# The last output-projection group, the second norm and the first MLP blocks in one written order

## The chip, the cores and the metric

The kernel runs on one NeuronCore of a Trainium2 chip. The metric is the device time of one execution in microseconds; the median of three runs stands for a kernel. TensorE (PE) does matrix products and writes PSUM, which has eight banks. VectorE (DVE) and ScalarE (ACT) do elementwise work, GpSimd (POOL) some additions and DMA issues, SyncE (SP) issues most DMAs. Each engine works through its own queue in order and waits on semaphores for the others.

## The reference

One layer of a transformer with two token mixers. For this change only its middle counts:

```python
x = x + g1 * (_merge_heads(o_da, o_mla, subln_w[l], lambda_init) @ w_o[l])
h2 = _modulate(_rmsnorm(x, norm2_w[l]), sh2, s2)
x = x + g2 * _conv_ffn(h2, w_up[l], conv_w[l], conv_b[l], w_down[l])
```

The modulation vectors (`g1`, `sh2`, `s2`, `g2` and others) are products of `silu(c)` with the 12288 columns of `w_ada`. `_conv_ffn` multiplies by `w_up`, passes the gate half through a centred convolution of width 3 over the tokens and a SiLU, multiplies by the other half, and multiplies by `w_down`. All is float32; 512 tokens, width 2048, feed-forward width 5632.

## The kernel before

Activations lie with features on the 128 partitions and the 512 tokens along the free dimension; a tensor of width 2048 is 16 tiles, numbered `kt` or `dt`. Each float32 product is done as three float32r products: an operand is split into a high part (a copy on ACT that rounds) and a low part (the difference, on DVE), and `mm3` (L104 to L109) adds high by high, high by low and low by high. `wblock` loads a block of weights (128 x 1024) on SP and splits it into `wh` and `wl`, of each of which there are three buffers.

**The output projection** (from L1101) has four groups of four output tiles, and in each group eight blocks of weights; one block is 24 matmuls of 512 columns. Groups 0 and 2 sum up in the two big PSUM tiles, groups 1 and 3 in four one-bank tiles. Between the blocks `next_gemv` computes modulation entries: it loads a row of `ada` (1 MB) and sums its product with `silu(c)` in one DVE instruction (L174). After a group, DVE evicts each output tile, scaled and with the residual added (L1120), into `x1`; POOL sends it to DRAM, ACT squares it, and POOL adds the squares into `ss`.

**The second norm** (`token_norm`, L1086) runs once for all 512 tokens behind the last group: ones matmuls sum `ss` and the last four squares over the partitions, and `rstd` (L160) takes the inverse root with two ACT instructions and four on DVE, one behind the other.

**The MLP's first two feature pairs** (`first_pair`, L1189) are done in the plain way: eight blocks of weights (`w_up0`), in the order 0, 4, 1, 5, 2, 6, 3, 7, each with two input tiles `kt`. For each tile, `normed` (L1152) multiplies by the norm on DVE and makes high and low parts for the two token halves; then `classical` multiplies, half by half, into four outputs: 48 matmuls of 256 columns to a block. From the third pair of features on, `w_up` is applied by a Strassen scheme; its fixed operands `t1` to `t4` are sums of normed tiles, built by `sums(j)` (L1165) for eight `j`, with some twelve DVE and ACT instructions each. The third pair itself is done plainly once more, in four jobs "u" (u0 to u3, 48 matmuls of 256 columns each). Then the "p" jobs begin (first at 1084.88 us in the trace), seven to a feature tile.

Up to and with `first_pair` (L1101 to L1205) the order of instructions here is the scheduler's: it may move each engine's instructions against one another. The jobs stand in `tc.manual_schedule`, where each engine's instructions keep the order of the program text. There, weights are split two jobs ahead: `cast(i + 2)` (ACT) and `low(i + 2)` (DVE) follow job `i`. `convolve`, `silu`, `multiply` and `finish` end the first two features in the order that the scheduler chose, beside the u jobs.

Of the kernel before, what the change touches and what calls it, by code (L numbers as in the profile page):

```python
# [17 lines left out]
P = 128  # L18
# [34 lines left out]
def layer_kernel(ctx: ExitStack, tc: tile.TileContext, small, rope, c_row, cc_row, x_t, ctx_t, ada, ada_k,  # L53
# [1009 lines left out]
    aq_ = tc.alloc_tile_pool(name="aq2", bufs=16, side="right", reuse_waits="tile")  # L1063

    def q2k(dt=F32):
        return aq_.tile([P, 512], dt, tag="q2k", name=nm("q2k"))

    wo = tc.alloc_tile_pool(name="wo", bufs=1, reuse_waits="tile")
# [4 lines left out]
    for h in range(16):  # L1073
        hl = a2k(F32R), q2k(F32R)
        split(hl[0], hl[1], oraw[h])
        osp.append(hl)

    def add_square(pool, ss, x, first):
        if first:
            sc.square(ss, x)  # L1080
        else:
            q = pool.tile([P, T], F32, tag="sq", name=nm("sq"), bufs=2)[:, :x.shape[1]]
            sc.square(q, x)
            gp.tensor_tensor(out=ss, in0=ss, in1=q, op=ALU.add)

    def token_norm(pool, ss, last):  # L1086

        n = ss.shape[1]
        po = b_tile()[:, :n]
        pe.matmul(po, ones32, ss, start=True, stop=False)  # L1090
        for i, x in enumerate(last):
            q = pool.tile([P, T], F32, tag="h", name=nm("sq"), bufs=5)[:, :n]
            sc.square(q, x)
            pe.matmul(po, ones32, q, start=False, stop=i == len(last) - 1)
        r = pool.tile([P, T], F32, tag="nr", name=nm("nr"), bufs=1)[:, :n]
        t1, t2 = (pool.tile([P, T], F32, tag="h", name=nm("n"), bufs=5)[:, :n] for _ in range(2))
        rstd(r, po, D, t1, t2)
        return r

    x1, ss = [], wo.tile([P, T], F32, name="ss")  # L1100
    for g in range(4):  # L1101
        if g % 2:
            outs = [b_tile() for _ in range(4)]
        else:
            s0, s1 = s_tile(), s_tile()
            outs = [s0[:, :512], s0[:, 512:], s1[:, :512], s1[:, 512:]]
        for kb in range(8):
            if kb > 2 and g == 0 or g in (1, 2) or kb < 7 and g == 3:
                next_gemv(wo, 1)
            wh, wl = wblock(w_o[g, kb])  # L1110
            order = [(j, i) for j in range(2) for i in range(4)]
            for j, i in sorted(order, key=lambda t: t[1]) if kb == 7 else order:
                kt, o = kb * 2 + j, j * 512 + i * P
                mm3(outs[i], (wh[:, o:o + P], wl[:, o:o + P]), osp[kt], kt == 0, kt == 15)
        for i in range(4):
            dt = g * 4 + i
            xr = wo.tile([P, T], F32, tag="xr", name=nm("xr"), bufs=6)
            nc.sync.dma_start(xr, x_t[dt])
            x = b2k()
            ve.scalar_tensor_tensor(out=x, in0=outs[i], scalar=modx[:, 32 + dt:33 + dt], in1=xr,  # L1120
                                    op0=ALU.mult, op1=ALU.add)
            x1.append(x)
            gp.dma_start(x1_d[dt], x)
            if g < 3:
                add_square(wo, ss, x, dt == 0)
# [5 lines left out]
    wo.release()  # L1131
    ps_b.release()
    ps_s.release()
    nb[0] = 3
    ps_b = ctx.enter_context(tc.tile_pool(name="ps_m", bufs=4, space=PSUM, reuse_waits="tile"))

    ff = tc.alloc_tile_pool(name="ff", bufs=1, reuse_waits="tile")
    hp = tc.alloc_tile_pool(name="hp", bufs=1, side="right", reuse_waits="tile")
    h0, h1 = slice(0, HT), slice(HT, T)
    r = token_norm(hp, ss, x1[12:])
# [3 lines left out]


    hf, hx, t1, t2, t3, t4 = ([None] * KT for _ in range(6))  # L1150

    def normed(kt):  # L1152

        b = modx[:, 48 + kt:49 + kt]
        h = hf[kt] = hp.tile([P, T], F32, tag="h", name=nm("h"), bufs=5)
        ve.scalar_tensor_tensor(out=h, in0=x1[kt], scalar=a2[:, kt:kt + 1], in1=r, op0=ALU.mult, op1=ALU.mult)
        hx[kt] = (a2k(F32R), q2k(F32R) if kt >= 8 else hp.tile([P, T], F32R, tag="h12", name=nm("h12"), bufs=8))
        for t, c in zip(hx[kt], (h0, h1)):
            hh, hl = half(t)
            sc.activation(hh, h[:, c], AF.Identity, bias=b)  # L1160
            ve.scalar_tensor_tensor(out=hl, in0=h[:, c], scalar=b, in1=hh.bitcast(F32), op0=ALU.add, op1=ALU.subtract)

    spare = [tp.tile([P, T], F32R, tag="tp", name=nm("tp")) for _ in range(8)]

    def sums(j):  # L1165

        a, c, b = hf[j], hf[j + 8], modx[:, 56 + j:57 + j]
        d1, d2 = (hp.tile([P, HT], F32, tag="d", name=nm("d"), bufs=2) for _ in range(2))

        def put_away(t, src):  # L1170
            t[j] = q2k(F32R) if t is t1 else spare.pop(0) if spare else b2k(F32R)
            split(*half(t[j]), src)

        ve.scalar_tensor_tensor(out=d1, in0=c[:, h1], scalar=db[:, j:j + 1], in1=a[:, h1], op0=ALU.add, op1=ALU.add)
# [505 lines left out]
```

## Time and profile before

| | us |
|---|---|
| median of three runs | 2394.99 |
| lowest and highest | 2392.95 and 2395.71 |
| the profiled execution | 2392.88 |
| its span in the profile | 2391.1 |

In the profile a line of the timeline gives start and duration in microseconds, the engine, the source line, the operation, output and inputs with their shapes, and in brackets the idle time of the engine ahead of it with what ended that. The view by stretches gives for each stretch its length and every engine's busy time with its number of instructions, then TensorE's granted clock (1.00 is full), the DMA engines' busy share and the rate. In the view by groups the last columns are busy time, mean duration in ns, and idle time ahead with what ended it. TensorE's records overlap: the distance from one to the next counts, not the duration.

### The profile page before, as it was taken

How to read it: one execution, taken by the hardware profiler on the slowest of the kernel's cores; microseconds unless marked ns; L12 is line 12 of the kernel's file. 1: busy time of each engine (PE TensorE's matmuls, PEld its weight loads, DVE VectorE, ACT ScalarE, POOL GpSimd, SP SyncE). 2: the span in 40 equal slices, each digit the busy share in tenths (PEclk: the TensorE clock that was granted, in tenths of full speed). 3: DMA queues.
4: the chain of work that ended last, by engine and by line, in shares of the span. 5: the costliest groups of instructions: out<-in, count | busy, mean ns of one | idle time of the engine just before them, and what ended most of it. 6: DMA issues, size and time to landing. Idle time of an engine off the chain costs nothing.

```text
span 2391.1 us, 32351 instructions
## 1 busy us (share of the span) xinstructions
PE 2331.0 (97%) x12444; PEld 1961.2 (82%) x12444; DVE 1778.5 (74%) x2303; ACT 1100.7 (46%) x1660; POOL 270.2 (11%) x322
## 2 busy tenths in 40 slices
PE   8999999999899999999999999999999999999997
PEld 5787888777677788798888888888888888888887
DVE  5996886798877877697585858575757676767767
ACT  4322322455555622364454545454545454445453
POOL 0011000121100011200101010101010101011113
PEclk9999999999999999999999999999999999999999
DMA  9767777853301289623646464546555545465572
GB/s 382 284 217 279 297 295 282 234 151 110 132 30 49 71 309 359 211 79 125 156 127 150 123 150 128 143 128 142 139 141 138 145 123 151 123 159 123 144 212 76
DMA packets 141515, 407.45 MB, mean 170 GB/s; under 512 B 14881, under 2 KB 31793, under 8 KB 130737
## 3 DMA queue, kind: packets, MB, share of 16 engines
q1 hardware_dynamic: 107584, 300.51, 37.9%
q0 software_dynamic: 32624, 103.83, 18.1%
q8 instruction: 97, 1.59, 0.3%
q10 hardware_dynamic: 1152, 1.05, 0.1%
q14 instruction: 58, 0.47, 0.1%
HBM read 335.86 MB, written 69.48 MB: 170 GB/s over the span
## 4 chain that ended last, share of the span: by engine, by line
PE 85%; DVE 8%; ACT 3%; issue 3%; DMA 1%; POOL 1%; DVEq 0%; SPq 0%; ACTq 0%; POOLq 0%
PE y L1377 13%; PE b L107 10%; PE b L108 10%; PE b L109 10%; PE z L1377 6%; PE y L1379 6%; PE z L1379 3%; PE s L883 3%; PE s L108 3%; PE s L107 3%; PE s L109 3%; PE x L1377 2%; PE x L1379 1%; PE pt L895 1%; PE f L107 1%
## 5 line engine op out<-in xcount | busy, mean ns | idle before, releaser
L1398 POOL DMA_DIRECT2D x_d<-xs x160 | 140.7, 1017 | 1160.4 <-ACT xs L1397 1140.8
L107 PE MATMUL b<-ah,wh 128*128 128x512 f32 (+1 forms) x672 | 259.1, 386 | 0.0
L108 PE MATMUL b<-al,wh 128*128 128x512 f32 (+1 forms) x672 | 259.0, 385 | 0.0
L109 PE MATMUL b<-ah,wl 128*128 128x512 f32 (+1 forms) x672 | 258.0, 384 | 0.0
L1353 DVE TENSOR_TENSOR wl<-rb,wh 128x1024 fp32r<-128x1024 f32 x124 | 151.2, 1220 | 128.7 <-ACT wh L1347 128.7
L1353 DVE TENSOR_TENSOR wl<-wr,wh 128x1024 fp32r<-128x1024 f32 x126 | 153.8, 1221 | 123.0 <-ACT wh L1347 123.0
L1347 ACT CAST wh<-wr 128x1024 fp32r<-128x1024 f32 x126 | 132.3, 1050 | 200.9 <-PE b L108 100.5
L1347 ACT CAST wh<-rb 128x1024 fp32r<-128x1024 f32 x124 | 130.2, 1051 | 191.7 <-PE b L108 116.1
L1353 DVE TENSOR_TENSOR wl<-ws,wh 128x1024 fp32r<-128x1024 f32 x123 | 150.1, 1221 | 89.2 <-ACT wh L1347 89.2
L174 DVE CUSTOM_DVE_ANT_0 ada<-ada,cb,smt 128x2048 f32<-128x2048 f32 x64 | 154.3, 2413 | 50.9 <-DMA ada<-in_ada 50.6
L1347 ACT CAST wh<-ws 128x1024 fp32r<-128x1024 f32 x123 | 128.3, 1043 | 135.7 <-PE b L108 45.4
L109 PEld LDWEIGHTS b<-ah,wl 128*128 128x128 f32 x672 | 126.3, 188 | 25.5
L107 PEld LDWEIGHTS b<-ah,wh 128*128 128x128 f32 x672 | 126.6, 188 | 22.9
L108 PEld LDWEIGHTS b<-al,wh 128*128 128x128 f32 x672 | 126.6, 188 | 22.0
L107 PE MATMUL b<-a2k,wh 128*128 128x512 f32 (+1 forms) x352 | 134.5, 385 | 7.3 <-ACT a2k L1160 5.0
L109 PE MATMUL b<-a2k,wl 128*128 128x512 f32 (+1 forms) x352 | 132.7, 377 | 0.7 <-DVE wl L402 0.6
L80 ACT CAST wh<-wr 128x1024 fp32r<-128x1024 f32 (+2 forms) x64 | 64.3, 1004 | 147.2 <-DMA wr<-in_w_o 45.7
L1377 PE MATMUL y<-b2k,wh 128*128 128x512 f32 x410 | 106.8, 390 | 0.0
L885 DVE TENSOR_REDUCE m<-s 128x1 f32<-128x768 f32 x96 | 90.2, 949 | 20.0 <-PE s L883 19.7
L81 DVE TENSOR_TENSOR wl<-wr,wh 128x1024 fp32r<-128x1024 f32 (+2 forms) x64 | 79.9, 1249 | 29.7 <-ACT wh L80 29.2
L1397 ACT ACTIVATE xs<-b,modx 128x512 f32<-128x512 f32 x160 | 101.0, 680 | 0.1
L210 ACT CAST wh<-wr 128x1024 fp32r<-128x1024 f32 x38 | 40.0, 1052 | 127.8 <-PE b L109 46.3
(536 smaller groups left out, 6080.5 us busy)
## 6 DMA issues: line engine op xcount, KB each, us to landing
rb<-in_w_up SPq DMA_DIRECT2D x123, 512.0 KB, 4.4
ada<-in_ada POOLq DMA_DIRECT2D x52, 1024.0 KB, 6.1
wr<-in_w_dn SPq DMA_DIRECT2D x84, 512.0 KB, 4.0
x_d<-xs POOLq DMA_DIRECT2D x160, 256.0 KB, 6.1
ada<-in_ada SPq DMA_DIRECT2D x28, 1024.0 KB, 6.9
wr<-in_w_up SPq DMA_DIRECT2D x53, 512.0 KB, 4.2
wr<-in_w_f SPq DMA_DIRECT2D x34, 512.0 KB, 5.9
adak<-in_ada_k SPq DMA_DIRECT2D x64, 256.0 KB, 5.4
```

The source lines that it names most:

```text
L81: ve.tensor_tensor(dst_l, src, dst_h.bitcast(F32), op=ALU.subtract)
L107: pe.matmul(out, st[0], mv[0], start=start, stop=False, **kw)
L108: pe.matmul(out, st[0], mv[1], start=False, stop=False, **kw)
L109: pe.matmul(out, st[1], mv[0], start=False, stop=stop, **kw)
L174: ve.tensor_tensor_reduce(out=junk, in0=w, in1=vec, op0=ALU.mult, op1=ALU.add, scale=1.0, scalar=col("b_ada", j), accum_out=dst[:, j:j + 1])
L885: ve.tensor_reduce(out=m, in_=s[:, :TT], axis=AX.X, op=ALU.max, negate=True)
L1347: sc.copy(hi, raw)
L1353: ve.tensor_tensor(lo, raw, hi.bitcast(F32), op=ALU.subtract)
L1377: pe.matmul(o, w[j][0], hs[j], start=start and j == 0, stop=False, skip_group_check=True)
L1379: pe.matmul(o[:, h0], w[j][1], hs[j][:, h0], start=False, stop=j == 7, skip_group_check=True)
L1397: sc.mul(x, po, modx[:, 80 + dt:81 + dt])
L1398: gp.dma_start(x1_d[dt], x, accum_op=ALU.add)
```

## The change

Three parts, all between the output projection and the p jobs.

*Written order.* The output projection's last group, the norm and the first pairs' blocks (now called units 0 to 7) stand in `tc.manual_schedule` for all engines. Seven rows of `ada` are summed within blocks 0 to 5, each row asked for two sums ahead. The weights of the last group, of the units and of u0 and u1 form one list `src8`; a block is cast and split two ahead (`cast8`, `low8`) and its load is asked for three ahead.

*Norm by token halves.* Blocks 6 and 7 of the last group run first for tokens 0 to 255, then for 256 to 511; `squares_of`, `ones_of`, `root_of` and `normed` take a half. Units 0 and 1 also run by halves.

*Places.* The units sum up in banks of the two big PSUM tiles and one more, apart from the last group's four; low parts lie in two pools of eight tiles; scratch tiles come from a pool `xsp`; the ring of the pairs' weights (`rb`) is allocated and first asked for after u2. `sums(j)` is cut into two steps, `first` (four differences on DVE, four copies on ACT) and `second` (four low parts on DVE), and `some(n)` issues the next n of the sixteen steps. `cast(2)` and `low(2)` stand ahead of the convolutions, `cast(3)` behind them.

```diff
+    def out_block(outs, kb, w, c=slice(0, T), skip=True):
+        order = [(j, i) for j in range(2) for i in range(4)]
+        for j, i in sorted(order, key=lambda t: t[1]) if kb == 7 else order:
+            kt, o = kb * 2 + j, j * 512 + i * P
+            mm3(outs[i][:, c], [t[:, o:o + P] for t in w], [t[:, c] for t in osp[kt]], kt == 0, kt == 15, skip)
...
+    def low8(i):
+        ve.tensor_tensor(hl8[i][1], raw8.pop(i), hl8[i][0].bitcast(F32), op=ALU.subtract)
+        load8(i + 3)
...
-    for g in range(4):
+    for g in range(3):
...
+    def normed(kts, *cs):
+        for kt in kts:
+            norm_in(kt, cs)
+        for kt in kts:
+            norm_low(kt, cs)
...
+        def first():
+            d1, d2, d3, d4 = ds[:] = [d for _ in range(2) for d in half(scratch())]
...
+            for t, d in zip((t1, t2, t3, t4), ds):
+                sc.copy(half(t[j])[0], d)
+
+        def second():
+            for t, d in zip((t1, t2, t3, t4), ds):
+                hh, hl = half(t[j])
+                ve.tensor_tensor(hl, d, hh.bitcast(F32), op=ALU.subtract)
...
+        for i in range(6):
+            out_block(outs, i, hl8.pop(i))
+            cast8(i + 2)
+            low8(i + 2)
+            for _ in range(1 + (i == 2)):
+                row_sum()
+                row_load()
+            if i == 2:
+                xrs = [residual(12 + k) for k in range(4)]
...
+        for kb in (6, 7):
+            out_block(outs, kb, hl8[kb], h0)
...
+        cast8(8)
+        low8(8)
+        squares_of(h0)
+        out_block(outs, 6, hl8[6], h1)
+        ones_of(h0)
+        out_block(outs, 7, hl8[7], h1)
+        root_of(h0)
+        normed(pair(0), h0)
+        squares_of(h1)
...
+        fo.append(b_tile())
+        unit(0, (h0,))
+        ones_of(h1)
+        cast8(9)
+        low8(9)
+        normed(pair(1), h0)
+        unit(1, (h0,))
+        cast8(10)
+        low8(10)
+        root_of(h1)
+        normed(pair(0), h1)
+        unit(0, (h1,))
+        normed(pair(1), h1)
+        cast8(11)
+        low8(11)
+        unit(1, (h1,))
+        normed(pair(2), h0, h1)
...
+        for n_ in range(2, 8):
+            unit(n_, (h0, h1))
+            cast8(10 + n_)
+            if n_ < 7:
+                normed(pair(n_ + 1), h0, h1)
+            low8(10 + n_)
+            some((0, 1, 2, 1, 2, 3)[n_ - 2])
...
+        for i in range(2):
+            ready[i] = *hl8.pop(16 + i), None, None
+        cast(2)
+        low(2)
+        for i in range(2):
+            t = convolve(i, fo[2 * i])
+            if i:
+                some(1)
+            acts[i] = multiply(silu(t), fo[2 * i + 1])
+            some(1 - i)
+            finish(t, acts[i])
...
         for i, job in enumerate(jobs[:last]):
             run(i)
+            if i == 2:
+                hp.release()
...
+                rb = Ring(mm, "rb", 3, items_b)
+                rb.pump()
...
-            cast(i + 2)
             if i:
+                cast(i + 2)
+            if i > 2:
                 act_after(i - 1)
                 vec_after(i - 1)
-            low(i + 2)
+            if i:
+                low(i + 2)
+            if i < 4:
+                some((2, 1, 0, 2)[i])
```

More of the change, by code (lines that the diff above doesn't have):

```diff
@@ L1073, in layer_kernel @@
     for h in range(16):
-        hl = a2k(F32R), q2k(F32R)
+        hl = a2k(F32R), q2k(h // 8, F32R)
         split(hl[0], hl[1], oraw[h])
         osp.append(hl)
[L1078 to L1098, printed above, removed]
@@ L1102, in layer_kernel, with load8, cast8 @@
+    raw8, hl8 = {}, {}
+    def load8(i):
+        if i < len(src8):
+            raw8[i] = wraw(src8[i])
+    def cast8(i):
+        hl8[i] = [wp.tile([P, 1024], F32R, tag=g, name=nm(g), bufs=3) for g in ("wh", "wl")]
+        sc.copy(hl8[i][0], raw8[i])
+    def low8(i):
+        ve.tensor_tensor(hl8[i][1], raw8.pop(i), hl8[i][0].bitcast(F32), op=ALU.subtract)
+        load8(i + 3)
+    x1, ss = [], wx.tile([P, T], F32, name="ss")
+    for g in range(3):
         if g % 2:
@@ L1152, in normed @@
[L1152 to L1161, printed above, removed]
```

214 lines of the change are left out of this document (136 added, 78 removed).

## The prediction

> **What bounds the kernel now.** I read the page first, then the stretches around the changed code, then the timeline in the one place where TensorE stops, and last the engines beside it.
>
> ```profile
> PE 2331.0 (97%) x12444; PEld 1961.2 (82%) x12444; DVE 1778.5 (74%) x2303; ACT 1100.7 (46%) x1660; POOL 270.2 (11%) x322
> PE 85%; DVE 8%; ACT 3%; issue 3%; DMA 1%; POOL 1%; DVEq 0%; SPq 0%; ACTq 0%; POOLq 0%
> ```
>
> TensorE is busy 97% of the span and carries 85% of the chain that ended last. So a change can win only where PE stops or runs slowly, and it loses wherever it makes PE stop. The stretches below run from the end of block 5 of the output projection's last group (two blocks before 1001.79) to the first Strassen job.
>
> ```profile
> core 0: us, PE busy (x) PEld busy (x) DVE busy (x) ACT busy (x) POOL busy (x), PEclk, DMA share, GB/s
> 990.91:1001.79 10.88, 10.88 (x49) 9.01 (x48) 4.59 (x5) 2.11 (x3) 1.22 (x3) 1.00 0.35 102
> 1001.79:1012.12 10.33, 4.73 (x12) 1.64 (x10) 6.07 (x9) 4.99 (x9) 0.97 (x2) 0.96 0.41 149
> 1012.12:1061.84 49.72, 49.33 (x386) 49.11 (x387) 48.30 (x103) 29.97 (x64) 0.00 (x0) 0.94 0.22 64
> 1061.84:1084.88 23.04, 23.04 (x193) 23.04 (x193) 17.63 (x30) 11.09 (x18) 0.00 (x0) 1.00 0.45 160
> ```
>
> ```profile
> 1012.10:1018.00 5.90, 5.88 (x27) 5.86 (x28) 5.87 (x14) 3.47 (x9) 0.00 (x0) 0.50 0.00 1
> ```
>
> Three things are to be seen. First, 1001.79 to 1012.12 is the second norm: PE works 4.73 of 10.33 us. Second, right behind it 27 matmuls take 5.90 us at a granted clock of 0.50, so 0.22 us each, where the four "u" jobs run 192 in 23.04 us, 0.12 us each. Third, from 1012.12 to 1061.84 DVE is busy 48.30 of 49.72 us: behind the norm **VectorE has no room**, though PE does not wait for it yet.
>
> PE's bare work from 1001.79 to 1084.88 is 576 matmuls at 0.12 (69.1) and the ones matmuls (4.3: eight records took 3.70, below), together 73.4 of 83.1 us. **9.7 us are lost**, and that is all that can be won.
>
> ```profile
> 1000.63 0.75 DVE L1120 SCALAR_TENSOR_TENSOR b2k<-b,modx,xr 128x512 f32<-128x512 f32 x1 [0.61 <-PE b L109]
> ...
> 1003.39 3.70 PE L1094 MATMUL b<-sq,ones 128*128 128x512 f32 x8 [0.57 <-ACT sq L1093]
> ...
> 1007.13 0.69 ACT L162 ACTIVATE nr<-b,epst 128x512 f32<-128x512 f32 x1 [2.23 <-PE b L1094]
> 1007.85 0.63 ACT L163 ACTIVATE nr<-nr 128x512 f32<-128x512 f32 x1
> 1007.85 0.69 DVE L164 TENSOR_SCALAR n<-b 128x512 f32<-128x512 f32 x1 [3.79 <-ACT nr L162]
> ...
> 1009.96 0.69 DVE L167 SCALAR_TENSOR_TENSOR nr<-n,nr 128x512 f32<-128x512 f32 x1
> 1010.77 1.42 DVE L1156 SCALAR_TENSOR_TENSOR h<-b2k,a,nr 128x512 f32<-128x512 f32 x2
> 1011.55 0.51 ACT L1160 ACTIVATE a2k<-h,modx 128x256 fp32r<-128x256 f32 x1 [3.08 <-DVE h L1156]
> ```
>
> Read downwards this is the stall: the last ones record, two ACT steps and four DVE steps of 0.63 to 0.69 us one behind the other, one norm multiply (0.75), one activation (0.51), and then PE (1012.12).
>
> **The change, part by part.** All times are on the clock of this execution. The zero of the hand schedule is 990.91. An instruction on a busy engine counts by its distance to the next, taken from these rows (DVE first, then ACT).
>
> ```profile
> 1050.54 0.75 DVE L1156 SCALAR_TENSOR_TENSOR h<-b2k,a,nr 128x512 f32<-128x512 f32 x1
> 1051.21 1.22 DVE L1353 TENSOR_TENSOR wl<-wr,wh 128x1024 fp32r<-128x1024 f32 x1
> 1052.35 0.75 DVE L81 TENSOR_TENSOR b2k<-d,b2k 128x256 fp32r<-128x256 f32 x2
> 1053.02 0.48 DVE L1180 SCALAR_TENSOR_TENSOR d<-h,modx,d 128x256 f32<-128x256 f32 x1
> 1053.41 0.48 DVE L1161 SCALAR_TENSOR_TENSOR a2k<-h,modx,a2k 128x256 fp32r<-128x256 f32 x1
> ```
>
> ```profile
> 1020.72 1.05 ACT L80 CAST wh<-wr 128x1024 fp32r<-128x1024 f32 x1 [2.12 <-PE b L108]
> 1021.67 0.71 ACT L80 CAST tp<-d 128x256 fp32r<-128x256 f32 x2
> ```
>
> So on DVE: a 512-wide multiply 0.66, a weight's low part 1.14, a 256-wide low part 0.34 (subtract) or 0.40 (with scalar). On ACT: a weight cast 0.95, a 256-wide copy 0.30.
>
> *Halves on PE.* Blocks 6 and 7 become 96 matmuls of 256 columns for 48 of 512: 96 × 0.12 = 11.52 for 10.88, so +0.64. The ones matmuls are cut in two at the same total. Unit 0 and unit 1 have the same matmuls as before.
>
> *The norm of the first half.* Its eviction and squares lie beside block 6's second half, its chain beside block 7's. No 256-wide row of that chain exists. It lies between half of the full rows (0.35 a step) and the full rows (0.69); I take 0.46 to 0.50, by the 256-wide rows next to it (0.48, 0.51). The first ones end at 1001.7, the chain gives the first activation at 1005.4, and PE has worked up block 7 at 1004.6: **0.9 us of waiting and 0.4 for the low part, in place of 9.7**. The clock stays up.
>
> *What is late next.* The written order puts weight blocks between the norm steps. PE waits again: for the second pair's first half (its multiply stands on DVE behind low8(9), which waits for cast8(9) behind the second half's squares) 0.8 + 0.4; for the first pair's second half (root_of(h1) behind low8(10)) 2.2 + 0.4; for unit 2 (behind cast8(11), which needs unit 0's buffer) 0.9 + 0.4. With the first wait, and 0.4 of short ones, that is 6.4. PE ends unit 7 at 990.91 + 11.52 + 4.27 + 384 × 0.12 + 6.4 = 1059.2, against 1061.84: **−2.6 us**.
>
> *What the moved sums cost.* From here DVE decides. That a written order is kept, waits and all, this kernel's own written part shows:
>
> ```profile
> 1086.55 0.75 DVE L1219 SCALAR_TENSOR_TENSOR t<-y,smt,t 128x511 f32<-128x511 f32 x1 [4.08 <-ACT t L1214]
> ...
> 1088.01 1.21 DVE L1353 TENSOR_TENSOR wl<-ws,wh 128x1024 fp32r<-128x1024 f32 x1
> ```
>
> DVE stood idle 4.08 us for the convolution's input, and the low part written behind it came after it all the same. By that rule: at 1025.9 DVE has issued pair 2's norm. Up to unit 7's sums it still has five pairs (2 × 0.66 + 4 × 0.40 = 2.92 each, 14.6), six lows (6.8), five first halves of a sum (0.40 × 3 + 0.34 and 0.12 of dependence, 1.66 each, 8.3), four second halves (4 × 0.34, 5.4): 35.1 us, and some 2.4 us of waits for ACT. It is done at 1063.4, **4 us behind PE**. Then the written order is cast(2), convolution 0, a half sum, convolution 1, a half sum, the second activation, two more half sums, and only then cast(3), which job u3 needs. The scheduler's order in the old kernel had that weight's low part here:
>
> ```profile
> 1064.42 1.28 ACT L1226 ACT_TABLE_LOAD   x1
> 1065.72 0.63 ACT L1226 ACTIVATE t<-t 128x512 f32<-128x512 f32 x1
> ...
> 1074.35 1.23 DVE L1353 TENSOR_TENSOR wl<-wr,wh 128x1024 fp32r<-128x1024 f32 x1 [0.87 <-ACT wh L1347]
> ```
>
> ```profile
> L1236 DVE TENSOR_TENSOR al<-t,ah 128x512 fp32r<-128x512 f32 x2 | 1.4, 688 | 0.7 <-ACT ah L1232 0.7
> L1230 DVE TENSOR_TENSOR t<-t,b 128x512 f32<-128x512 f32 x2 | 1.4, 681 | 0.0
> L1219 DVE SCALAR_TENSOR_TENSOR t<-b,smt,t 128x511 f32<-128x511 f32 x1 | 0.7, 746 | 0.0
> L1353 DVE TENSOR_TENSOR wl<-wr,wh 128x1024 fp32r<-128x1024 f32 x3 | 3.7, 1225 | 0.9 <-ACT wh L1347 0.9
> ```
>
> It was 4.7 us ahead of u3 (1061.84 + 3 × 5.76 = 1079.1). In the new order DVE's work between 1063.4 and low(3) is: low(2) 1.1, four convolution steps 3.0, two products 1.3, two low parts 1.3, two first halves of a sum 3.3, two second halves 2.7: 12.7. DVE waits for ACT's casts, the table load (1.28), the two silus, the copies and the reuse of the one tile t, each 0.7 to 2.1: 8.0. So low(3) starts at 1084.1, its cast ends just before. PE asks for u3 at 1059.2 + 17.3 = 1076.5 and **stands 7.5 us, then 1.0 for the low part: +8.5**. Queued behind cast(3) on ACT are cast(4) and cast(5), and behind low(3) on DVE low(4), the weight sum and the last sum; the p jobs get them just in time, so I add nothing there (at most 1.1).
>
> *The clock.* The old stall had 5.03 us of idle PE and then 5.9 us at 0.50. 7.5 us of idle should do the same to u3: 5.9 / 2 = 2.95 us, of which about 1 lies in the wait for low(3): +2.0. The shorter waits (up to 2.2) I take at nothing; if one of them dropped the clock it would cost up to 2.95.
>
> By the Trainium skill ("TensorE: Matmul & The Clock Gate", Part 1) the clock halves after an idle window of about 3.4 us and returns after about as long a busy one. By its figure the u3 wait would cost an estimated 1.7 us in place of 2.95; the trace's 5.9 us at 0.50 is longer, and the measurement is used above.
>
> *Banks.* Evicting the first half reads a bank into which PE wants to write the second half. An eviction is 0.75 at full width; four end by 997.3, and PE comes back to each bank later than that (996.7 + 0.36 for each next bank, the first bank done 2 us earlier). Cost 0; if DVE began only after block 7's whole first half, under 1 us. The Trainium skill ("PSUM — Partial Sum Buffer", on bank collisions) forbids two engines on one bank at once, which speaks against halves in a bank; no wait of this kind is in the trace.
>
> *Rows.* Seven row sums lie in blocks 0 to 5.
>
> ```profile
> 978.77 2.35 DVE L174 CUSTOM_DVE_ANT_0 ada<-ada,cb,smt 128x2048 f32<-128x2048 f32 x1 [3.24 <-DMA ada<-in_ada]
> ```
>
> With a low part a block of 5.44 us holds 1.14 + 2.4 of DVE, so even a wait of 3.24 in front of a sum is caught up within two blocks, and weights are split two blocks ahead. So 0. The loads of u2 and u3 are asked for as low8(15) and low8(16) free their buffers, more than a unit (5.76) ahead of their casts. The pairs' ring moves behind u2 on SP's queue:
>
> ```profile
> rb<-in_w_up SPq DMA_DIRECT2D x123, 512.0 KB, 4.4
> ```
>
> Its first use is the weight sum behind u3's start; asked for within u2, three loads at 4.4 us land before DVE, late as it is, comes to them: 0, and without that lateness up to some 3 us.
>
> **Sum**: −2.6 + 8.5 + 2.0 = **+7.9 us**. The profiled execution took 2392.88 (span 2391.1), low in the three runs (2392.95 to 2395.71); on their median, 2394.99, it gives **2402.9**.
>
> **Rivals.** *Faster.* The halves hide the norm and DVE, which starts its norm 6.4 us earlier (1004.4 for 1010.77), brings low(3) in by 1076.5. Without waits on ACT it would: 1084.1 less its waits (8.0 here, 2.4 in the units, some 5 before) is below 1070. Then −2.6 stands, which is no change yet; with the waits at the start half as long too (3.2 for 6.4) it is −5.8: about 2389; at the very best −9.7 + 0.64, 2386. For it speaks that DVE idled only 1.4 us in the 49.7 us above; against it, that there the scheduler mixed the sums freely, and the written order does not. It decides at low(3) = 1076.5.
>
> *No change.* DVE is not late, or by 2 to 5 us at most with PE's clock up, and this eats the gain at the front: 2392 to 2398.
>
> *Worse.* A short wait at the front drops the clock as well (+2.95) or the p jobs wait too (+1.1, DVE having little room behind): 2404 to 2407.
>
> *Not what it says.* If the rows or weights came late, PE would stop inside blocks 0 to 5, where it never stops now; it would be seen there, and would add to the forecast.
>
> **How the numbers follow.** The forecast (2399 to 2404 by itself) has 0.48, the worse case 0.12, no change 0.20, faster 0.20. About 0.2%, 4.8 us, is what a measurement of this kernel can tell from no change. Range 2387 to 2408: it takes in most of the faster case and all of the worse one.
>
> **What would show it.** Right: in the new profile PE waits under 1.5 us ahead of unit 0, in all 5 to 7 us before unit 2; PE ends unit 7 near 1059; then one wait of 6 to 9 us ahead of u3 on ACT's cast or DVE's low, with a granted clock near 0.5 behind it; DVE waits for ACT in the convolutions. Wrong: no wait ahead of u3, or low parts coming before the sums on DVE, or PE idle for rows in the last group.

## The result, and the profile after

| | before | changed |
|---|---|---|
| median, us (four runs each) | 2395.35 | 2412.93 |
| lowest and highest, us | 2392.95, 2396.84 | 2410.95, 2415.26 |
| span of the profiled execution, us | 2391.1 | 2409.2 |

The changed kernel is slower: ratio 1.0075, 95% interval 1.0057 to 1.0092. The direction was forecast, the size was not: 2402.9 was forecast, and 2412.93 lies outside the range of 2387 to 2408. Of the runs below, one execution of f1 (3894.68 us) and one of i1 (5388.43 us) were far slower than the rest and are left out of all figures.

On the page of the changed kernel the busy shares of the engines (its first line) are what they were. TensorE is busy 8.5 us longer, since it runs slowly in places, and no other engine became the bound of the whole. The loss has to be looked for in the stretch.

```profile
PE 2339.5 (97%) x12502; PEld 1971.3 (82%) x12502; DVE 1780.0 (74%) x2315; ACT 1101.2 (46%) x1666; POOL 268.7 (11%) x322
```

The stretch that the change touches runs from the first matmul of block 6 to job p(4,0), from where the two kernels do the same. Its ends, from the timelines, first of before, then of after:

```profile
990.91 0.39 PE L107 MATMUL b<-a2k,wh 128*128 128x512 f32 x1
...
1104.36 2.00 PE L1377 MATMUL y<-a2k,wh 128*128 128x512 f32 x8
```

```profile
991.34 0.28 PE L107 MATMUL b<-a2k,wh 128*128 128x256 f32 x1
...
1122.76 1.55 PE L1485 MATMUL y<-a2k,wh 128*128 128x512 f32 x6
```

It is 113.45 us before and 131.42 us after: **+18.0**, and the spans differ by 18.1. So the whole loss is in here. This also gives a sharper measure than the total: what lies ahead of block 6 takes 990 to 1001 us from one profiled execution to the next, whatever is changed behind it, while two executions of one kernel agree in the stretch to 0.1 us (experiment h2 below, whose clock is full throughout). The experiments are therefore compared by the stretch first. Where a wait drops the clock, the stretch is less exact: what the same code takes can differ by 1.4 us from one execution to the next (e2 below).

Where the 18 us went is seen in the timeline of TensorE, cut to the matmuls that had to wait (in brackets the idle time ahead and what ended it), and in the view by stretches with the granted clock (the column behind POOL).

```profile
1005.75 0.38 PE L107 MATMUL s<-a2k,wh 128*128 128x256 f32 x1 [0.59 <-ACT a2k L1165]
...
1017.72 0.38 PE L107 MATMUL s<-h,wh 128*128 128x256 f32 x1 [2.38 <-ACT h L1165]
...
1079.22 0.55 PE L107 MATMUL z<-a2k,wh 128*128 128x256 f32 x1 [6.33 <-DVE t L1341]
...
1106.41 2.07 PE L1485 MATMUL y<-b2k,wh 128*128 128x512 f32 x4 [7.70 <-ACT m L1409]
```

```profile
1017.72:1022.50 4.78, 4.64 (x24) 4.45 (x25) 2.54 (x6) 1.26 (x3) 0.00 (x0) 0.66 0.00 0
...
1026.12:1061.21 35.09, 34.95 (x289) 34.76 (x289) 32.64 (x66) 19.71 (x41) 0.00 (x0) 1.00 0.28 89
...
1079.22:1092.96 13.74, 13.74 (x96) 13.74 (x97) 8.57 (x16) 3.73 (x7) 0.00 (x0) 0.82 0.39 140
...
1106.41:1111.58 5.17, 5.17 (x16) 4.40 (x17) 4.67 (x6) 2.62 (x3) 0.00 (x0) 0.52 0.21 53
```

Three waits, at unit 0's second half, at u2 and at p(3,2), and behind each of them a granted clock below 1. The old wait of 5.03 us at the norm is gone. Unit 7 ends 69.87 us behind the start of block 6 (1061.21), where it was 70.93: the norm's part wins 1.1 us. Job p(3,0) starts at 1092.96, 101.6 us behind block 6, for 93.8 before (in the old timeline its first matmul starts at 1084.71, not at 1084.88): 7.8 us have been lost by then. The other 10.2 go at p(3,2).

Below is the chain that ends at p(3,2), from the timelines of VectorE, ScalarE and SyncE's queue (SPq), in order of time.

```profile
1084.31 2.00 ACT L1455 CAST wh<-wr 128x1024 fp32r<-128x1024 f32 x2
1085.38 1.23 DVE L1461 TENSOR_TENSOR wl<-wr,wh 128x1024 fp32r<-128x1024 f32 x1 [1.95 <-ACT wh L1455]
...
1086.64 0.33 SPq L1366 DMA_DIRECT2D wr<-in_w_up  x1
...
1087.02 1.37 SPq L1366 DMA_DIRECT2D rb<-in_w_up  x3
...
1091.67 1.23 DVE L1425 TENSOR_TENSOR ws<-rb,wr 128x1024 f32<-128x1024 f32 x1 [2.58 <-DMA rb<-in_w_up]
...
1094.21 1.05 ACT L1455 CAST wh<-rb 128x1024 fp32r<-128x1024 f32 x1 [7.91 <-DMA rb<-in_w_up]
1095.30 1.22 DVE L1461 TENSOR_TENSOR wl<-rb,wh 128x1024 fp32r<-128x1024 f32 x1 [2.40 <-ACT wh L1455]
...
1100.92 1.04 ACT L1455 CAST wh<-ws 128x1024 fp32r<-128x1024 f32 x1 [1.79 <-DVE ws L1428]
...
1105.78 0.58 ACT L1409 COPY m<-y 128x512 f32<-128x512 f32 x1
```

Read it downwards. low(3) runs at 1085.38. When it has read its buffer, SyncE may refill that buffer (the `wr` load at 1086.64). The three loads of the pairs' ring stand behind this load in SyncE's order and go out at 1087.02. ScalarE then stands 7.91 us and VectorE 2.58 us for their data, and everything that is written behind them (a sum, the second weight sum, the third convolution, the copy `m` that frees the tile of p(3,2)) comes as much later. In the old kernel the same loads went out 15 us earlier, and ahead of the refills:

```profile
1071.91 1.81 SPq L1259 DMA_DIRECT2D rb<-in_w_up  x3
...
1073.82 0.87 SPq L1259 DMA_DIRECT2D wr<-in_w_up  x2
```

My theory, at this point: two chains, one behind the other. The written order of VectorE and ScalarE makes cast(3) and low(3) late, and u2 or u3 waits; and through SyncE's order the late low(3) makes the pairs' loads late, and p(3,2) waits. The rival for u2: the wait names `t` of L1341, the second product, and u2's output tile lies in the PSUM bank (4) in which that product still reads `fo[3]`; so a bad bank alone may be the cause. The `z` tile that the change asks for first, to move u2's tile one slot on, is written and read by nothing, and u2 waits as if it were not there.

### The profile page after: what moved, and what is told of

Same layout as the page of the kernel before. It is cut to its first block, busy times and chain, and to the rows that moved or that the text cites. A ratio compares the mean times of both kernels' runs of the same rounds, so it can differ in the third digit from the quotient of the medians.

```text
span 2409.2 us, 32462 instructions
## 1 busy us (share of the span) xinstructions
PE 2339.5 (97%) x12502; PEld 1971.3 (82%) x12502; DVE 1780.0 (74%) x2315; ACT 1101.2 (46%) x1666; POOL 268.7 (11%) x322
## 4 chain that ended last, share of the span: by engine, by line
PE 84%; DVE 8%; ACT 4%; issue 2%; DMA 1%; POOL 1%; SPq 0%; DVEq 0%; ACTq 0%; POOLq 0%
PE y L1485 13%; PE b L107 10%; PE b L108 10%; PE b L109 10%; PE z L1485 6%; PE y L1487 6%; PE s L108 3%; PE s L109 3%; PE s L107 3%; PE z L1487 3%; PE s L883 3%; PE x L1485 2%; PE x L1487 1%; PE pt L895 1%; PE f L107 1%
## 5 line engine op out<-in xcount | busy, mean ns | idle before, releaser
L109 PE MATMUL b<-ah,wl 128*128 128x512 f32 (+1 forms) x672 | 258.0, 384 | 0.0
L174 DVE CUSTOM_DVE_ANT_0 ada<-ada,cb,smt 128x2048 f32<-128x2048 f32 x57 | 135.8, 2385 | 48.6 <-DMA ada<-in_ada 48.4
L109 PEld LDWEIGHTS b<-ah,wl 128*128 128x128 f32 x672 | 126.3, 188 | 25.6
L107 PE MATMUL b<-a2k,wh 128*128 128x512 f32 (+1 forms) x336 | 128.8, 383 | 0.1
L109 PE MATMUL b<-a2k,wl 128*128 128x512 f32 (+1 forms) x336 | 125.9, 375 | 0.0
L80 ACT CAST wh<-wr 128x1024 fp32r<-128x1024 f32 (+2 forms) x50 | 49.6, 991 | 111.2 <-DMA wr<-in_w_o 60.3
L1485 PE MATMUL y<-b2k,wh 128*128 128x512 f32 x328 | 85.7, 404 | 11.2 <-ACT m L1409 11.2
L107 PE MATMUL s<-a2k,wh 128*128 128x512 f32 (+1 forms) x240 | 89.7, 374 | 1.5 <-ACT a2k L1165 1.5
```

What stands on the lines that cost most here:

```text
L107: pe.matmul(out, st[0], mv[0], start=start, stop=False, **kw)
L109: pe.matmul(out, st[1], mv[0], start=False, stop=stop, **kw)
L174: ve.tensor_tensor_reduce(out=junk, in0=w, in1=vec, op0=ALU.mult, op1=ALU.add, scale=1.0, scalar=col("b_ada", j), accum_out=dst[:, j:j + 1])
L1485: pe.matmul(o, w[j][0], hs[j], start=start and j == 0, stop=False, skip_group_check=True)
```

## The experiments

"Stretch" in the tables is from unit 0's start to job p(4,0): 117.0 us in the changed kernel. From block 6 to unit 0's start they take 14.4 us (h2's two executions 14.6 and 14.7), so that the old kernel's 113.45 from block 6 stands against 99.0 here. Runs of one table row are compared with runs of the kernel before on the same chip.

### The causes taken one by one

**e1: the bank.**

```diff
-                    live["s"] = [b_tile(g_, 2) for g_ in "yz"]
+                    live["s"] = [b_tile("y", 2), b_tile()]
```

> Only u2's and u3's output tile goes from bank 4 (where fo[3], the second gate product's input, still lies) to bank 0. Theory (the order of ScalarE and VectorE sets the end: cast(3) and low(3) stand behind both convolutions, and the pairs' loads behind low(3) on SyncE's queue): the 6.3 us wait ahead of u2 goes, a wait of 7 to 8 us ahead of u3 takes its place, the wait of 7.7 us ahead of p(3,2) stays, and the time stays within 2 us of the changed kernel, 2411 to 2415. Rival (the bank that u2 shares with fo[3] is the cause of the loss there): the wait goes and nothing comes in its place, 2404 to 2407.

**e2: SyncE's order.** The load that low(3) sets free is asked for behind the three loads of the pairs' ring.

```diff
-        def low(i):
+        def low(i, hold=False):
...
-                if done:
+                if done and not hold:
                     done()
...
                 rb.pump()
+                ready[3][3]()
...
-                low(i + 2)
+                low(i + 2, i == 1)
```

> Only the load that low(3) sets free (it refills the ring of the u and w11 weights) is asked for behind the three loads of the pairs' ring on SyncE's queue, not ahead of them. Theory (the pairs' loads are late because they stand on SyncE's queue behind a load that waits for low(3)): they are issued some 4 to 5 us earlier, the wait of 2.6 us ahead of the first weight sum goes, the wait ahead of p(3,2) falls from 7.7 to 2 to 3 us, and the time by 4.5 to 7 us, to 2406 to 2408.5. Rival (VectorE's own order, the sums and low parts that stand ahead of the third convolution, holds p(3,2) back, and the loads wait beside it): p(3,2) still waits 6 us or more, 2411 to 2414.

**e3: cast(3) ahead of the second convolution**, with u2's tile away from `fo[3]`: the pool of the jobs' PSUM tiles is opened ahead of the last group, whose outputs, `po` and `fo` are now tiles of that pool.

```diff
+        outs = [b_tile(g_, 2) for g_ in "zzyy"]
...
+        po, *fo = [b_tile(*t) for t in (("b", 3), ("b", 3), ("b", 3), ("x", 1))]
...
+        fo.append(b_tile("z", 2))
...
+        run(0)
+        run(1)
         for i in range(2):
             t = convolve(i, fo[2 * i])
...
             finish(t, acts[i])
+            if not i:
+                cast(3)
+                low(3)
```

> The cast and low part of u3's weight go ahead of the second convolution, and the output tiles lie so that u2 shares no bank with fo[3]. Theory (u2 and u3 wait only for these two things): PE runs from unit 7 through u3 without a wait over 1 us and at full clock, u3 ends 8 to 10 us earlier, p(3,2) still waits 6 to 8 us for the copy behind the third convolution, since VectorE's work in front of it is the same, and the time falls by 6 to 9 us, to 2404 to 2407. Rival (VectorE is short of time as a whole, not in a bad order): what u3 gains is lost again ahead of p(3,2), whose wait grows to 12 us or more, and the time stays at 2411 to 2414.

**e4: the front.** The weight blocks of units 1 and 2 leave the places ahead of norm steps.

```diff
         out_block(outs, 6, hl8[6], h1)
+        cast8(9)
+        low8(9)
         ones_of(h0)
...
         ones_of(h1)
-        cast8(9)
-        low8(9)
...
-        cast8(10)
-        low8(10)
         root_of(h1)
         normed(pair(0), h1)
         unit(0, (h1,))
+        cast8(10)
+        low8(10)
```

> In the norm's part the cast and low part of unit 1's weight go ahead of the first half's root (ScalarE waits for the ones matmuls there), and those of unit 2's weight behind unit 0's second half. Theory (two weight blocks written ahead of norm steps make the waits of 0.4 and 2.4 us, and the 2.4 us wait halves the clock): PE waits at most 1 us in any place from block 6 to unit 2, the granted clock stays at 1.00, unit 7 ends 3.5 to 5.5 us earlier, and since everything behind is shifted the time falls by as much, to 2407.5 to 2409.5. Rival (the waits only move to unit 1's second half and unit 2): unit 7 ends less than 1.5 us earlier, 2411.5 to 2414.

| | median, us | ratio to before (95%) | stretch, us | wait at u2, u3 | wait at p(3,2) |
|---|---|---|---|---|---|
| e1_bank | 2415.02 | 1.0076 (1.0059 to 1.0094) | 116.6 | 2.49, then 2.55 + 0.75 | 6.83 |
| e2_ring | 2408.02 | 1.0048 (1.0030 to 1.0065) | 108.2 | 6.34, none | 3.16 |
| e3_cast3 | 2409.29 | 1.0046 (1.0027 to 1.0064) | 109.2 | none | 7.50 |
| e4_front | 2409.96 | 1.0061 (1.0041 to 1.0080) | 116.0 | 6.42, none | 7.45 |

*e1* decides between theory and rival. TensorE's waits in its timeline:

```profile
1079.01 0.35 PE L107 MATMUL b<-a2k,wh 128*128 128x256 f32 x1 [2.49 <-DVE t L1332]
1089.04 0.39 PE L107 MATMUL b<-a2k,wh 128*128 128x256 f32 x1 [2.55 <-ACT wh L1455]
1090.30 0.58 PE L109 MATMUL b<-a2k,wl 128*128 128x256 f32 x1 [0.75 <-DVE wl L1461]
```

u2 still waits a little, now for the first convolution, whose input lies in its new bank, and u3 waits for cast(3) and low(3), 3.3 us in place of the 7 to 8 expected. The stretch wins 0.4 us. The bank is what the trace names, and it costs next to nothing by itself: behind it stands the order, ready to take the same time.

*e2*: the pairs' loads go out at 1067.58 in its trace, 71.5 us behind block 6 where it was 95.7, and no instruction waits for them any more:

```profile
1067.58 2.60 SPq L1366 DMA_DIRECT2D rb<-in_w_up  x3
1090.07 0.33 SPq L1366 DMA_DIRECT2D wr<-in_w_up  x1
```

```profile
1104.67 2.12 PE L1485 MATMUL y<-b2k,wh 128*128 128x512 f32 x8 [3.16 <-ACT m L1409]
```

The wait at u2 is as it was, the one at p(3,2) falls from 7.70 to 3.16, and the clock stays at 1.00 behind it. The stretch is 8.8 us shorter, but not all of this is the edit's. From p(3,0) to p(4,0) it takes 22.98 us for 29.80, which is 6.8 less. Another 1.4 were won ahead of unit 2, in code that the edit leaves alone: behind the same wait of 2.38 us the clock stayed at 1.00 in this execution (last section), and unit 0's second half and unit 1's took 7.02 us for 8.40. The last 0.6 came behind the u2 wait, at a clock of 0.87 for 0.82. So of the 18.0 us lost, 6.8 were the place of one load on one queue. The ratio says about the same (1.0048 for 1.0075, 6.5 us), and the median came within the 2406 to 2408.5 expected.

*e3*: u2 and u3 do not wait, p(3,0) waits 1.26, and p(3,2) waits 7.50, though the pairs' loads went out 24.6 us ahead of it and nothing waits for them:

```profile
1079.89 1.37 SPq L1370 DMA_DIRECT2D rb<-in_w_up  x3
```

```profile
1104.47 3.78 PE L1489 MATMUL y<-b2k,wh 128*128 128x512 f32 x8 [7.50 <-ACT m L1413]
```

That is the second half of the theory: VectorE's work ahead of the third convolution is late by itself. The stretch falls by 7.8, as expected, 0.5 of it at the front, where unit 0's second half waits 1.72 us for 2.38 (`po` has a tile of its own here, see e4). The median shows less (1.0046), and block 6 started 6 us later in this execution than in the changed kernel's.

*e4* missed. The 0.39 us wait at unit 1 went, the 2.4 us wait stayed to the hundredth, unit 7 ended 1.3 us earlier, and the stretch won 1.0 us, where 3.5 to 5.5 were expected. The timeline shows why: ScalarE's first root step of the second half

```profile
1012.61 0.48 ACT L162 ACTIVATE nr<-s,epst 128x256 f32<-128x256 f32 x1 [3.74 <-PE s L109]
```

waits for L109, a matmul of a unit, though its sums are ready when the ones matmuls end, at 1008.89 + 1.89 = 1010.78. `po` and `fo[0]` are the two halves of one PSUM tile, `s`, and the step waits for all that is written to this tile ahead of it in the program, unit 1's first half too.

### The front with po in a tile of its own, and both together

**f1** is e4's front with e3's tiles (`po` alone in a tile, u2 away from `fo[3]`). **f2** is f1 with e3's early cast(3).

> The weight blocks are moved as in e4_front, and the sums of squares (po) have an output tile of their own, not one half of the tile whose other half takes unit 0's first result; u2's tile lies apart from fo[3] too. Theory (ScalarE's first root step of the second half waits for the tile that unit 1's first half writes, not only for its own sums): that step starts within 0.3 us of the last ones matmul, the wait of 2.4 us ahead of unit 0's second half falls to 0.3 to 0.8 us, the granted clock stays at 1.00 behind it, unit 7 ends 4.5 to 6 us earlier counted from unit 0's start, and the stretch from unit 0's start to job p(4,0), 117.0 us in the changed kernel and 116.0 in e4_front, falls to 111 to 112.5. Rival (the root step waits for something else, the order on its queue or the ones matmuls themselves): the wait stays at 2 us or more and the stretch at 115 to 116.5.

> The front of f1_front_po and the earlier cast of u3's weight of e3_cast3 together. If the front and the middle are separate losses they add: 111.8 expected for the front, 7.8 less for the middle, so 103 to 105.5 us from unit 0's start to p(4,0), with one wait of 6 to 8 us left ahead of p(3,2). Rival (VectorE has no room, so that PE's earlier units only wait for it later): 107 or more, and the wait ahead of p(3,2) grows to 10 us.

| | median, us | ratio to before (95%) | stretch, us | wait at unit 0's second half | at u3 | at p(3,2) |
|---|---|---|---|---|---|---|
| f1_front_po | 2410.82 | 1.0055 (1.0033 to 1.0078) | 113.0 | 0.59 | 6.81 + 0.46 | 6.48 |
| f2_all | 2403.22 | 1.0030 (1.0015 to 1.0044) | 106.1 | 0.59 | none | 7.49 |

In f1 the root step follows the ones matmuls at once, and the clock stays up where the changed kernel had 0.66:

```profile
1018.67 1.89 PE L1273 MATMUL b<-sq,ones 128*128 128x256 f32 x8
```

```profile
1020.60 0.48 ACT L162 ACTIVATE nr<-b,epst 128x256 f32<-128x256 f32 x1 [1.96 <-PE b L1273]
```

```profile
1024.01:1029.00 4.99, 4.71 (x32) 4.11 (x33) 3.90 (x8) 3.14 (x5) 0.00 (x0) 1.00 0.22 71
```

So the wait had two causes, either of which was enough for most of it: the shared tile alone made 2.38 us (e4), the weight blocks ahead of the root alone 1.72 (e3). f1 missed its sum all the same: unit 7 ended 3.9 us earlier (4.5 to 6 expected), and the stretch is 113.0 (111 to 112.5 expected), since u3 now waits 7.3 us in two pieces for cast(3) and low(3). f2 lies between theory and rival (106.1, for 103 to 105.5 or 107 and more): front (4.0) and middle (7.8) nearly add up to the 10.9 that it wins, and the wait at p(3,2) stays. With everything mended that is in one place, the written order still loses 7 us against the kernel before.

### The rest left to the scheduler

**h1** keeps f1's front by hand up to unit 1. Units 2 to 7, the sums and the first two convolutions stand outside `manual_schedule`, and the written order starts at u0 as in the kernel before.

```diff
-        for n_ in range(2, 8):
-            unit(n_, (h0, h1))
...
+    for n_ in range(2, 8):
+        if n_ > 3:
+            cast8(8 + n_)
+            low8(8 + n_)
+        for j, kt in enumerate(pair(n_)):
+            if n_ > 2:
+                normed([kt], h0, h1)
+            if n_ % 2 == 0:
+                some(2)
+            for i in range(4):
+                o = j * 512 + i * P
+                classical(fo[i], kt, [t[:, o:o + P] for t in hl8[8 + n_]], False, n_ == 7 and j == 1)
+    some(4)
...
+    for i in range(2):
+        t = silu(convolve(i, fo[2 * i]))
+        acts[i] = finish(t, multiply(t, fo[2 * i + 1]))
```

**h2** is h1 with four sums among the units in place of six, one in each of units 4 to 7, and the other four behind the convolutions.

```diff
-            if n_ % 2 == 0:
+            if (n_, j) in ((4, 1), (5, 1), (6, 1), (7, 1)):
                 some(2)
...
         acts[i] = finish(t, multiply(t, fo[2 * i + 1]))
+        some(4)
```

**h3** is h1 with the low parts of the sums on GpSimd, and **h4** has both edits.

```diff
-                ve.tensor_tensor(hl, d, hh.bitcast(F32), op=ALU.subtract)
+                gp.tensor_tensor(out=hl, in0=d, in1=hh.bitcast(F32), op=ALU.subtract)
```

> The front of f1_front_po by hand up to unit 1; units 2 to 7, the sums, the two convolutions and u0's and u1's weights are left to the scheduler, and the written order begins at job u0 as in the kernel before. Theory (the written order of sums, weights and convolutions makes the loss behind the front; VectorE has the time, given the scheduler's mixing): PE does not wait over 1 us anywhere from unit 2 to p(4,0), the stretch from unit 0's start to p(4,0) is 93 to 96 us (92.2 in the kernel before, whose norm stands ahead of it), and with the 9.7 us at the norm cut to some 3 the kernel is faster than before by 3 to 7 us, ratio 0.997 to 0.999. Rival (VectorE, idle for only 1.4 of 49.7 us in the units of the kernel before, is the bound as soon as PE's norm wait goes): PE waits 3 to 6 us spread over units 2 to 7, the stretch is 97 to 100 us, and the time equals before within 0.1%.

> As h1_hybrid (102.3 us from unit 0's start to p(4,0), waits of 1.2 to 1.5 us ahead of four units, VectorE busy 5.00 of 5 us from 1030 to 1060), but two sums fewer stand among the units: they come behind the convolutions, where VectorE had idle time in h1_hybrid (2.56 and 3.92 of 5 us busy from 1080 to 1090). Theory (VectorE has no room in the units and PE waits for it there; it has room behind them): the waits ahead of the units fall below 0.5 us each, the stretch to 96 to 99 us, the ratio to before to 0.999 to 1.001. Rival (VectorE is short over the whole stretch to p(4,0)): the waits come back in jobs u0 to p(3,3), the stretch stays at 101 us or more.

> As h1_hybrid, with the 32 low parts of the sums (0.34 us each on VectorE, 10.9 us in all) done by GpSimd, whose 256-wide two-input operation takes 0.80 us in the kernel before and which has nothing else to do there. Theory (VectorE's work is the bound from the norm to the p jobs): PE's four waits of 1.2 to 1.5 us go, the stretch from unit 0's start to p(4,0) falls from 102.3 to 94 to 97 us, the kernel is faster than before by 2 to 5 us, ratio 0.998 to 0.999. Rival (the waits come from the order and from latency between ScalarE and VectorE, not from VectorE's load): the stretch stays at 100 us or more.

> h2_later and h3_pool together. Theory (VectorE's load): no more than 1 us better than the better of the two, since either makes room enough: 94 to 96 us from unit 0's start to p(4,0), ratio 0.9975 to 0.999. Rival (GpSimd, 32 x 0.80 = 25.6 us of work, becomes late when the sums start later): p(3,2) to p(3,5) wait for low parts on GpSimd, 98 us or more.

| | median, us | ratio to before (95%) | stretch, us |
|---|---|---|---|
| h1_hybrid | 2399.82 | 1.0022 (1.0009 to 1.0034) | 102.3 |
| h2_later | 2389.82 | 0.9965 (0.9953 to 0.9977) | 95.7 |
| h3_pool | 2403.92 | 1.0026 (1.0013 to 1.0039) | 104.5 |
| h4_both | 2398.53 | 1.0009 (0.9998 to 1.0021) | 101.2 |

*h1* missed what the theory expected, 93 to 96, and what the rival did. Its units and its u jobs, from the view by stretches (behind PE and PEld the third busy time is VectorE's):

```profile
1024.42:1074.91 50.49, 44.20 (x336) 42.48 (x337) 48.85 (x108) 29.77 (x64) 0.00 (x0) 0.97 0.23 71
1074.91:1097.95 23.04, 23.04 (x194) 23.04 (x193) 15.77 (x22) 9.98 (x14) 0.00 (x0) 1.00 0.46 166
```

VectorE is full in the units (48.85 of 50.49) and has 7.3 us to spare behind them. TensorE waits 1.2 to 1.5 us ahead of four units for a norm step, and its clock is 0.97 on the mean. So VectorE is the bound, but only there. *h2* says that this reading is right: with two sums moved into the room behind, no wait is left behind unit 2, the stretch is 95.7, and in this run the kernel is faster than before. Its units from unit 2 on and its u jobs:

```profile
1022.76:1057.46 34.70, 34.70 (x288) 34.70 (x289) 34.70 (x74) 20.87 (x45) 0.00 (x0) 1.00 0.29 95
1057.46:1080.50 23.04, 23.04 (x194) 23.04 (x193) 19.98 (x38) 12.31 (x22) 0.00 (x0) 1.00 0.43 146
```

*h3* took 10.9 us of work from VectorE and won nothing: the ratio is the same as h1's, and the stretch is 2.2 us longer in the one execution traced of each (94 to 97 was expected, 104.5 came). About 1.7 of these 2.2 are a second fall of the clock to 0.66 for 5 us. VectorE stays full, 51.48 of 52.56 us in the units, with 78 instructions for h1's 108. From the view by groups, the norm's multiply in the units, first h1, then h3, and h3's low parts on GpSimd (POOL):

```profile
L1162 DVE SCALAR_TENSOR_TENSOR tp<-b2k,a,nr 128x512 f32<-128x512 f32 x6 | 4.2, 745 | 0.0
```

```profile
L1162 DVE SCALAR_TENSOR_TENSOR tp<-b2k,a,nr 128x512 f32<-128x512 f32 x6 | 7.2, 1217 | 0.0
```

```profile
L1203 POOL TENSOR_TENSOR b2k<-xs,b2k 128x256 fp32r<-128x256 f32 x16 | 16.5, 1037 | 13.7 <-ACT b2k L1198 13.7
```

While GpSimd works on two tensors, VectorE's multiply takes 1217 ns for 745. Inside h3's trace the same is seen: the multiply that meets a step of GpSimd takes 1.22 us, the next one, with GpSimd idle from 1038.4 to 1041.9, 0.73.

```profile
1036.35 2.06 POOL L1203 TENSOR_TENSOR b2k<-xs,b2k 128x256 fp32r<-128x256 f32 x2
```

```profile
1036.59 1.22 DVE L1162 SCALAR_TENSOR_TENSOR tp<-b2k,a,nr 128x512 f32<-128x512 f32 x1
...
1039.81 0.73 DVE L1162 SCALAR_TENSOR_TENSOR q2k<-b2k,a,nr 128x512 f32<-128x512 f32 x1
```

GpSimd's own step takes 1037 ns, for 803 of an addition of the same size in the kernel before:

```profile
L1523 POOL TENSOR_TENSOR ss<-ss,sq 128x256 f32<-128x256 f32 x26 | 20.9, 803 | 51.4 <-ACT sq L1521 50.2
```

The work left VectorE, the time did not. The Trainium skill says this ("GPSIMD Engine Reference", "1. Specifications"): GpSimd shares its SBUF interfaces with VectorE, and there is contention with VectorE's instructions that have two SBUF inputs. The trace agrees, with 0.47 us for each multiply. *h4* shows it from the other side: with the sums moved, GpSimd's help makes 95.7 into 101.2 (94 to 96 was expected); u2 waits 2.07 us there for its weight's low part on VectorE.

### The last two waits

**i1** is h2 with the front's norm steps ahead of the weights of units 2 and 3; h2 ran again beside it.

```diff
-        cast8(10)
-        low8(10)
         normed(pair(1), h1)
-        cast8(11)
-        low8(11)
-        unit(1, (h1,))
+        cast8(10)
+        low8(10)
         normed(pair(2), h0, h1)
+        cast8(11)
+        low8(11)
+        unit(1, (h1,))
```

> As h2_later, but in the written front the norm of unit 1's second half and of unit 2's pair stands ahead of the weight blocks of units 2 and 3. Theory (the weight blocks make the two waits that are left there, 0.53 us for unit 0's second low part and 1.42 us ahead of unit 2): both go, and the stretch from unit 0's start to p(4,0), 95.7 us in h2_later, falls to 93.5 to 94.5. Rival (VectorE is full there, so the wait only moves to the weight's low part): 95 to 96.5.

> h2_later once more, beside i1_pairs on one chip: 95.7 us from unit 0's start to p(4,0), ratio to before 0.996 to 0.999 (the stretch alone is 3.3 us shorter than in the kernel before, which would be 0.9986).

| | median, us | ratio to before (95%) | stretch, us |
|---|---|---|---|
| i1_pairs | 2389.59 | 0.9972 (0.9960 to 0.9984) | 93.1 |
| h2_again | 2393.74 | 0.9996 (0.9982 to 1.0010) | 95.7 |

```profile
1012.40:1021.55 9.15, 8.43 (x58) 7.76 (x58) 6.88 (x17) 4.27 (x11) 2.16 (x4) 1.00 0.30 116
1021.55:1062.78 41.23, 40.70 (x336) 40.50 (x337) 41.23 (x85) 25.36 (x52) 0.00 (x0) 1.00 0.30 90
1062.78:1085.82 23.04, 23.04 (x194) 23.04 (x193) 22.39 (x45) 13.46 (x26) 0.00 (x0) 1.00 0.45 158
```

The wait ahead of unit 2 went, the 0.53 us for unit 0's second low part stayed. VectorE is now full in the units and nearly full in the u jobs, TensorE is busy 40.70 of 41.23 and then without a gap, and the clock is 1.00 throughout. i1 is faster than both kernels: its stretch is 5.9 us shorter than before's, and the ratio says the same (0.28% of 2394.9 are 6.7). h2's two intervals do not overlap, while its stretch was 95.7 both times; counted from block 6, it is 3.0 to 3.1 us better than before. So the ratio moves by more than its interval from one row of runs to the next, and the stretch is the better witness.

## Why the prediction was right or wrong, point by point

- **The bound and what can be won.** Right: TensorE, with 9.7 us to win at the norm and VectorE without room behind it. i1 won 5.9 of them.
- **The front, −2.6.** The waits came as forecast. (The prediction's own terms, four waits with their low parts and 0.4 of short ones, add to 6.8, not to its 6.4.) From block 6 to unit 7's end 69.87 us passed, for 61.87 us of bare work (11.52 + 4.27 + 46.08), so 8.0 were lost, where 6.4 of waits were forecast; the sum was −1.1. The term that was too small is "The shorter waits (up to 2.2) I take at nothing": behind the wait of 2.38 the clock was 0.66 over 4.78 us, which is the 1.6 us that make the difference. In e2, with the same front, this cost did not come, so it is partly chance. The cause of the wait was named by half: low8(10) stood ahead of the root, but the shared tile makes the same wait without it (e4, f1).
- **VectorE 4 us late, low(3) at 1084.1.** Right, and in its parts too. low(3) ran at 1085.38, 0.9 us late when counted from block 6. Though written ahead of low(2), two of unit 7's three sum steps ran behind it (below, from 1063.67 on), and the first convolution step ran among them:

```profile
1062.54 1.22 DVE L1461 TENSOR_TENSOR wl<-wr,wh 128x1024 fp32r<-128x1024 f32 x1
1063.67 0.42 DVE L1203 TENSOR_TENSOR q2k<-xs,q2k 128x256 fp32r<-128x256 f32 x1
...
1066.80 0.48 DVE L1195 SCALAR_TENSOR_TENSOR xs<-tp,modx,xs 128x256 f32<-128x256 f32 x1
```

  Unit 7's sums were done at 1067.19. Without low(2) (1.13 us) and that step (0.66), which belong to what follows, this would be 1065.4, 4.2 us behind TensorE (1061.21). From there to low(3) VectorE took 20.0 us, 7.3 of them waits for ScalarE and 12.7 of work, where 20.7 were forecast, 8.0 of waits and 12.7 of work.
- **One wait ahead of u3, +8.5, and +2.0 of clock.** The place was wrong and the time a little too long: 6.33 us ahead of u2 and none ahead of u3, then 0.82 over 13.74 us, which costs 2.5 us, so 8.8 for 10.5. "Banks: cost 0" looked at the last group's banks only and not at u2's tile beside `fo[3]`; e1 shows that this changed the place of the wait and not the sum. At p(3,0) the loss was 7.8 us, and the forecast of the whole change was 7.9; that they are so close is luck, since 1.5 us too little at the front stands against 1.7 too much here.
- **The step that failed: the pairs' ring at 0, the p jobs at nothing.** The prediction took the ring's loads as asked for within u2 and landed in time, "0, and without that lateness up to some 3 us", and the p jobs as getting their weights "just in time, so I add nothing there (at most 1.1)". It saw that the ring moved behind u2 on SyncE's queue, but not that a load ahead of it there waits for low(3), the very instruction that it had forecast as late. What came was a wait of 7.70 us at p(3,2) and a clock of 0.52 for 5.17 us behind it: +10.2. e2 undid the queue's order alone and gave 6.8 of it back. The other 3.4 are VectorE's own order: in e2 p(3,2) still waits 3.16 us, and in e3 7.50, with the loads there in time.
- **Rows, halves on PE.** No wait showed in blocks 0 to 5 and none for banks in blocks 6 and 7. Block 6 to unit 0 took 14.41 us, of which 0.59 was waiting.
- **The rivals.** "Faster" decided at low(3) by 1076.5, and it came at 1085.38. "Worse" had both of the right parts, a clock drop at the front and waiting p jobs, at 2.95 and 1.1 us; the second was nine times too small.

## What to carry to other kernels

A late instruction is late for everyone behind it on every in-order queue: when a chain is forecast late, follow what it sets free, the refill of its buffer too, and what is queued behind that refill. A wait that the trace names need not be a cost: undo it alone (e1) before mending it, since another may stand right behind. And where one engine is full in one stage and idle in the next, moving work between the stages won 6.6 us here (h1 to h2), while moving it to an engine that slows the full one won nothing (h1 to h3).

## What the runs showed of the hardware

A short wait can drop the clock, and its length does not tell whether it does. Behind the 2.38 us at unit 0's second half it was 0.66 over the next 4.78 us in the changed kernel (above), 0.64 in e1 and 0.70 in e4. In e3, behind 1.72 us at the same place, it was 0.66:

```profile
1023.04:1028.00 4.96, 4.82 (x25) 4.62 (x26) 2.54 (x6) 1.27 (x4) 0.00 (x0) 0.66 0.05 20
```

In e2, whose front is written as in the changed kernel and shows the same waits, it stayed at 1.00 behind the 2.38 us, and again behind the 3.16 us at p(3,2):

```profile
1022.52 0.38 PE L107 MATMUL s<-h,wh 128*128 128x256 f32 x1 [2.38 <-ACT h L1165]
```

```profile
1022.52:1027.30 4.78, 4.64 (x36) 4.44 (x37) 2.79 (x7) 2.31 (x4) 0.00 (x0) 1.00 0.00 0
1104.67:1110.37 5.70, 5.70 (x32) 5.02 (x33) 5.70 (x7) 3.71 (x5) 0.00 (x0) 1.00 0.25 83
```

The Trainium skill ("TensorE: Matmul & The Clock Gate", Part 1) has the clock halve after an idle window of about 3.4 us. Here it fell behind waits of half that length, and stayed up behind one of nearly the whole of it. Since one and the same front went both ways, the written order alone does not decide it; what the gate counts was not tried.
